# Feed-forward stage of a float32 decoder block: ACT, DVE and POOL in program order, with evacuations issued in steps and summed weight pages loaded from a list of their own

## The chip, the core and the metric

The kernel runs on one core of one Trainium2 chip. The metric is the device time of one execution in microseconds (us), smaller being better. Engines are named as in the profile: PE multiplies matrices (PEld is its weight load), DVE is the vector engine, ACT the scalar engine, POOL is GpSimd, and SP issues the DMAs.

## The reference

One decoder layer over 256 tokens of width 1024, all in float32: a mixer (8 block-sparse heads, of which at this length only the block of the token itself counts, and 4 differential heads, both gated), then a SwiGLU feed-forward of width 2816, each between two RMS norms.

```python
h = rms_norm(x, norm_mix_pre_g)
mq, mk, mv, dq, dk, dv, ga, gb = split(h @ w_in)
ya = moba_attention(mq, mk, mv)            # softmax with ALiBi, 8 heads of 64
yb = rms_norm(diff_attention(dq, dk, dv))  # softmax1 - lam * softmax2, 4 heads of 128
merged = sigmoid(ga) * (ya @ w_branch_a) + sigmoid(gb) * (yb @ w_branch_b)
x = x + rms_norm(merged @ w_out, norm_mix_post_g)
h = rms_norm(x, norm_ffn_pre_g)
f = (silu(h @ w_gate) * (h @ w_up)) @ w_down
x = x + rms_norm(f, norm_ffn_post_g)
```

## The kernel before

**Products.** Every float32 operand is kept as two parts, a rounded part `hi` and the rest `lo`, and every product is three matmuls into one PSUM bank: hi·hi, hi·lo, lo·hi (`mm3`, lines 216 to 218). So each weight tile of 128x1024, here called a granule, is first split (`split_part`): ACT writes `whi` (line 184), then DVE writes `wlo` = raw − `whi` (line 187). There are five buffers for `whi` and five for `wlo`. A granule's split therefore waits until PE is done with the granule five before it, and PE waits for both parts of a granule.

**Slots and jobs.** A stage is a list of slots. A slot holds a few matmuls (`pe`), the granules that they need, and what follows them (`post`). Splits and weight sums are jobs in one list. `run` walks the slots: it first issues all jobs up to those that slots a few places ahead need (`AHEAD` = 4 slots), then the matmuls, then `post`, then one step of every generator in `active`.

**Order on the engines.** PE and SP always run in program order. ACT, DVE and POOL run in program order inside the block that `order` opens. Outside it a scheduler at build time sets their order. Before, the scheduler orders them from the 15th slot of the mixer on, and in the whole feed-forward; program order holds at the start of the kernel and between the two stages.

**Feed-forward.** The 22 chunks of 128 hidden columns are computed in this order: 4 chunks as natural products (`nat`), then units `R 4, W 6, R 10, W 12, R 16, W 18`. An R unit covers 2 chunks with four granules r0 to r3, each used for both halves of the tokens (12 matmuls of 512 columns per granule). A W unit covers 4 chunks with seven block products in place of eight, on sums of weight blocks and of blocks of h. In PE's order its blocks are 21, 11, T2, T1, T3, 22 and T4, with two granules each and 6 matmuls per granule. The sums T1 to T4 are eight adds on DVE (line 268) over *pages* of 128x1024. The pages are loaded from HBM; twelve are in use, and a page is loaded anew when its last user is done. The sums of h (`s_step`: two adds, four half adds, two splits into `S`) are made once.

**From a unit to its down projection.** PE's result is evacuated from PSUM (R: SiLU on ACT, then a product on DVE, called `fr`, lines 1074 and 1075; W: `q1` to `q7`, ending in `f` of the first tokens, lines 1044 and 1045, and `f` of the second, lines 1049 and 1050). `f_T` transposes it on PE into the single bank `t` and splits the bank into `fT` hi (ACT) and `fT` lo (DVE). Then the down projection adds it into four `acc` banks: one granule per chunk, d0 to d21, 18 matmuls each (`z_slots`). PE's order in a unit is: first block or granule, transposes left over from the unit before, second block, down projection of the chunks before, the rest, and in a W unit the transposes of its first tokens. The last four chunks, d18 to d21, are split in halves and end the kernel (`z_tail`). Two of them have buffers of their own, named `wextra`.

In the mixer, `ev_q` and `ev_k` evacuate the q and k projections: DVE reads a bank of `acc` (four in turn, `q<-acc,R` at line 528), and ACT and DVE split the result. PE reuses the bank two slots later.

Of the kernel before, what the change touches and what calls it, by code (L numbers as in the profile page):

```python
# [20 lines left out]
F32 = mybir.dt.float32  # L21
F32R = mybir.dt.float32r
# [43 lines left out]
def tile_hybrid_block(  # L66
# [77 lines left out]
    def load_raw(r):  # L144
        if r["home"] == "page":
            r["page"] = free.pop(0)
            t = page(r["page"], "wpage")
        else:
            t = wpool.tile([P, 1024], F32, tag="raw", name="wraw", bufs=RB)
            raw_home.append(r)  # L150
        r["flat"] = t
        r["tile"] = t.rearrange("p (a c) -> p a c", a=r["a"])
        cur["raw"] += 1

    def load_raws():
        while cur["raw"] < len(raw_order):
            r = raw_order[cur["raw"]]
            if r["home"] == "page":
                if not free:
                    break  # L160
            elif len(raw_home) >= RB and raw_home[-RB]["uses"] > 0:
                break
            load_raw(r)
            for c, v in r["views"]:
                nc.sync.dma_start(r["tile"][:, :, c], v)
# [126 lines left out]
    for ui, (kind, f0) in enumerate(UNITS):  # L292
        ds = [lambda i=i: job_split(("d", i), dr[i]) for i in units_before(ui)]
        if kind == "R":
            rr = [raw_of([(slice(0, 256), rows(w_gate, 2 * kc * P, 2, f0 * P, 256)),
                          (slice(256, 512), rows(w_up, 2 * kc * P, 2, f0 * P, 256))], 2) for kc in range(4)]
            rs = [lambda kc=kc: job_split(("r", f0, kc), rr[kc]) for kc in range(4)]
            ad = early_sums(UNITS[ui + 1][1])
            todo = rs[0:2]
            if ui == 0:  # L300
                sjobs = [raw_of([], 2, "page") for i in range(4)]
                todo += [lambda: (use(*sjobs), [add_job(lambda n=n: s_step(n)) for n in range(10)])]
            for i in range(max(len(ds), 2)):
                todo += ds[i:i + 1] + ad[i:i + 1]
            ad = ad[max(len(ds), 2):]
            todo += rs[2:3] + ad[0:1] + rs[3:4] + ad[1:]
# [20 lines left out]
    def run(slots, ahead, starts={}):  # L327
        need = [max([job_of[h] for h in s["need"] if h in job_of], default=0) for s in slots]
        for i, s in enumerate(slots):
            split_to(max(need[:i + 1 + ahead(i)], default=0))  # L330
            for th in starts.get(i, []):
                active.append(th)
            s["pe"]()
            for f in s.get("post", []):
                f()
            for th in list(active):
                try:
                    next(th)
# [604 lines left out]
    mean_sq(xt[:, 1, :], ms2[:, 1:2])  # L943
    split_next()
    nat(fg[1], "gn", 1, range(4, 8))
    order.__exit__(None, None, None)
    rs2 = rstd(ms2, 2, NORM_EPS, "rs1")
    free.extend([10, 11, 12, 13])
    load_raws()
# [10 lines left out]

        return fT[f, t]

    def f_T(fv, f0, n, t, tag="t"):

        def pe():
            b = ps(tag)
            for j in range(n):
                nc.tensor.transpose(b[:, j * P:(j + 1) * P], fv()[:, j * P:(j + 1) * P], ident)
            h, l = [v[:, 0:n * P] for v in (work.tile([P, 512], F32R, tag="q", name="fT", bufs=5) for _ in range(2))] \
                if n == 4 else (lambda v: [v[:, 0:n * P], v[:, 256:256 + n * P]])(  # L970
                    work.tile([P, 512], F32R, tag="q", name="fT", bufs=5))
            split(b[:, 0:n * P], h, l)
            for j in range(n):
# [38 lines left out]
    def unit_W(f0):  # L1012
# [6 lines left out]

        def slots_of(n, bk, a, start, stop, post):  # L1020
            return [dict(pe=lambda kp=kp: block(bank(bk), a, n, f0, kp, start, stop), need=[((n, f0, kp), 0)],
                         post=[post] if kp else []) for kp in range(2)]

        def q1():
            s1 = work.tile([P, 512], F32, tag="ph0", name="s1", bufs=1)
            nc.scalar.activation(s1, st["a"], AF.Copy)
            g = st["g0"] = work.tile([P, 512], F32, tag="e", name="g0", bufs=4)
            nc.vector.tensor_tensor(g, st["b"], s1, op=OP.add)
            nc.scalar.activation(g, g, AF.Silu, scale=rs2[:, 0:1])

        def q6():
            st["s2"] = work.tile([P, 512], F32, tag="ph0", name="s2", bufs=1)
            nc.scalar.activation(st["s2"], st["a"], AF.Copy)

        def q5():
            st["v5"] = work.tile([P, 512], F32, tag="pl0", name="v5", bufs=1)
            nc.scalar.activation(st["v5"], st["b"], AF.Copy)

        def q7():
            nc.vector.tensor_tensor(st["v5"], st["v5"], st["a"], op=OP.subtract)  # L1040

        def q3():
            u = st["f0"] = work.tile([P, 512], F32, tag="e", name="f0", bufs=4)
            nc.vector.tensor_tensor(u, st["b"], st["s2"], op=OP.subtract)
            nc.vector.tensor_tensor(u, u, st["g0"], op=OP.mult)

        def q4():
            g = st["f1"] = work.tile([P, 512], F32, tag="e", name="f1", bufs=4)
            nc.scalar.activation(g, st["a"], AF.Silu, scale=rs2[:, 1:2])
            nc.vector.tensor_tensor(g, g, st["v5"], op=OP.mult)  # L1050

        head = slots_of("21", "b", A(0, 1), True, True, lambda: None)
# [4 lines left out]
        body[1].append(f_T(lambda: st["f0"], f0, 4, 0))  # L1057
        return head, body[0], body[1], [f_T(lambda: st["f1"], f0, 4, 1)]

    def unit_R(f0):  # L1060
        st = []
# [10 lines left out]
        def done(t):  # L1072
            g = st[t]["f"] = work.tile([P, 512], F32, tag="e", name="fr", bufs=4)[:, 0:256]
            nc.scalar.activation(g, st[t]["b"][:, 0:256], AF.Silu, scale=rs2[:, t:t + 1])
            nc.vector.tensor_tensor(g, st[t]["b"][:, 256:512], g, op=OP.mult)

        sl = [dict(pe=lambda kc=kc, t=t: pe(kc, t), need=[(("r", f0, kc), 0)],
                   post=[lambda t=t: done(t)] if kc == 3 else []) for kc in range(4) for t in range(NT)]
# [21 lines left out]
    slots[-1]["post"] = [nat_mul]  # L1100
    left = [f_T(lambda t=t: fgs[t], 0, 4, t, "pv" if t else "t") for t in range(NT)]
# [56 lines left out]
```

## Time and profile before

| | |
|---|---|
| median of 3 runs | 398.88 us (396.45 to 399.57) |
| the profiled execution | 399.47 us, span 397.7 us |
| PE busy | 375.9 us, 95% of the span |
| DVE busy | 311.1 us, 78% |
| ACT busy | 234.2 us, 59% |
| DMA | 67.64 MB, 170 GB/s on average |

The span runs from the first to the last instruction; the execution's own time is 1.8 us longer. The profiled execution lies 0.6 us above the median. The mixer takes the first 196 us, the feed-forward the rest. PE's busy time is nearly the span, so the place to read is PE's idle time, and what ended it.

### The profile page before, as it was taken

How to read it: one execution, taken by the hardware profiler on the slowest of the kernel's cores; microseconds unless marked ns; L12 is line 12 of the kernel's file. 1: busy time of each engine (PE TensorE's matmuls, PEld its weight loads, DVE VectorE, ACT ScalarE, POOL GpSimd, SP SyncE). 2: the span in 40 equal slices, each digit the busy share in tenths (PEclk: the TensorE clock that was granted, in tenths of full speed). 3: DMA queues.
4: the chain of work that ended last, by engine and by line, in shares of the span. 5: the costliest groups of instructions: out<-in, count | busy, mean ns of one | idle time of the engine just before them, and what ended most of it. 6: DMA issues, size and time to landing. Idle time of an engine off the chain costs nothing.

```text
span 397.7 us, 6046 instructions
## 1 busy us (share of the span) xinstructions
PE 375.9 (95%) x2212; PEld 326.8 (82%) x2212; DVE 311.1 (78%) x523; ACT 234.2 (59%) x402; POOL 34.0 (9%) x51
## 2 busy tenths in 40 slices
PE   7998999999999999999999997989998989979993
PEld 5798989998999999998888885867876868858883
DVE  2798787989877667896899996599866799677934
ACT  3964675777556864571786435675354763467721
POOL 0199600000000000000010000000000000000000
PEclk9999999999999999999999998999998999989999
DMA  6998555354455554685079923568451669000002
GB/s 197 388 298 296 161 162 160 105 158 136 129 158 160 194 177 159 199 270 168 14 274 370 380 70 110 160 211 264 160 155 48 188 227 356 33 0 0 2 0 106
DMA packets 37855, 67.64 MB, mean 170 GB/s; under 512 B 2993, under 2 KB 15298, under 8 KB 37826
## 3 DMA queue, kind: packets, MB, share of 16 engines
q1 hardware_dynamic: 37826, 67.26, 51.4%
q8 instruction: 17, 0.28, 0.3%
q14 instruction: 12, 0.10, 0.1%
HBM read 66.20 MB, written 1.05 MB: 169 GB/s over the span
## 4 chain that ended last, share of the span: by engine, by line
PE 82%; DVE 7%; DMA 6%; issue 2%; ACT 2%; SPq 1%; DVEq 0%; POOLq 0%; ACTq 0%
PE acc L216 13%; PE acc L217 13%; PE acc L218 13%; PE s L216 9%; PE s L217 8%; PE s L218 8%; PE acc L589 5%; DVE wlo L187 4%; DMA wpage<-in_w_up_dram 2%; DMA wpage<-in_w_gate_dram 2%; PE pv L217 2%; PE pv L218 2%; PE pv L216 2%; ACT whi L184 2%; DMA xt<-in_x_dram 1%
## 5 line engine op out<-in xcount | busy, mean ns | idle before, releaser
L187 DVE TENSOR_TENSOR wlo<-wraw,whi 128x1024 fp32r<-128x1024 f32 (+1 forms) x105 | 114.9, 1106 | 22.9 <-ACT whi L184 20.5
L184 ACT ACTIVATE whi<-wraw 128x1024 fp32r<-128x1024 f32 (+1 forms) x104 | 98.6, 962 | 57.5 <-PE acc L217 23.4
L216 PE MATMUL acc<-hTh,whi 128*128 128x256 f32 x256 | 73.4, 287 | 1.8 <-DVE q L528 1.6
L218 PE MATMUL acc<-hTh,wlo 128*128 128x256 f32 x256 | 71.9, 281 | 0.0
L217 PE MATMUL acc<-hTl,whi 128*128 128x256 f32 x256 | 71.9, 281 | 0.0
L187 DVE TENSOR_TENSOR wlo<-wpage,whi 128x1024 fp32r<-128x1024 f32 x42 | 50.6, 1223 | 18.9 <-ACT whi L184 18.8
L184 ACT ACTIVATE whi<-wpage 128x1024 fp32r<-128x1024 f32 x42 | 44.1, 1060 | 32.4 <-PE pv L218 18.7
L216 PEld LDWEIGHTS acc<-hTh,whi 128*128 128x128 f32 x256 | 48.3, 189 | 2.5 <-DVE q L528 1.8
L217 PEld LDWEIGHTS acc<-hTl,whi 128*128 128x128 f32 x256 | 48.3, 189 | 0.0
L218 PEld LDWEIGHTS acc<-hTh,wlo 128*128 128x128 f32 x256 | 48.2, 188 | 0.0
L216 PE MATMUL s<-whi,h2h 128*128 128x512 f32 x92 | 39.4, 428 | 2.7 <-DVE v L1040 1.6
L217 PE MATMUL s<-wlo,h2h 128*128 128x512 f32 x92 | 38.2, 416 | 0.0
L218 PE MATMUL s<-whi,h2l 128*128 128x512 f32 x92 | 38.0, 413 | 0.0
L268 DVE TENSOR_TENSOR wpage<-wpage 128x1024 f32<-128x1024 f32 x24 | 29.1, 1219 | 5.8 <-DMA wpage<-in_w_up_dram 4.3
L216 PE MATMUL acc<-whi,fT 128*128 128x512 f32 (+1 forms) x80 | 29.2, 365 | 0.0
L218 PE MATMUL acc<-whi,fT 128*128 128x512 f32 (+1 forms) x80 | 29.1, 364 | 0.0
L217 PE MATMUL acc<-wlo,fT 128*128 128x512 f32 (+1 forms) x80 | 29.1, 364 | 0.0
L216 PEld LDWEIGHTS s<-whi,h2h 128*128 128x128 f32 x92 | 18.4, 200 | 8.5 <-ACT whi L184 2.0
L852 POOL TENSOR_TENSOR rs_r<-rs_e,mhalf 128x1 f32<-128x1 f32 x4 | 2.2, 546 | 235.6 <-DVE rs_e L851 235.6
L218 PEld LDWEIGHTS s<-whi,h2l 128*128 128x128 f32 x92 | 18.3, 199 | 4.5
L217 PEld LDWEIGHTS s<-wlo,h2h 128*128 128x128 f32 x92 | 18.3, 199 | 3.6
L218 PE MATMUL s<-whi,S 128*128 128x512 f32 x48 | 19.0, 395 | 0.0
(267 smaller groups left out, 763.5 us busy)
## 6 DMA issues: line engine op xcount, KB each, us to landing
wraw<-in_w_in_dram SPq DMA_DIRECT2D x37, 512.0 KB, 3.7
wraw<-in_w_down_dram SPq DMA_DIRECT2D x22, 512.0 KB, 5.8
wpage<-in_w_up_dram SPq DMA_DIRECT2D x12, 512.0 KB, 4.1
wpage<-in_w_gate_dram SPq DMA_DIRECT2D x12, 512.0 KB, 7.5
wraw<-in_w_out_dram SPq DMA_DIRECT2D x8, 512.0 KB, 3.4
wraw<-in_w_gate_dram SPq DMA_DIRECT2D x12, 256.0 KB, 6.0
wraw<-in_w_up_dram SPq DMA_DIRECT2D x12, 256.0 KB, 6.1
wraw<-in_w_branch_a_dram SPq DMA_DIRECT2D x4, 512.0 KB, 3.5
```

The source lines that it names most:

```text
L184: nc.scalar.activation(hi, src, AF.Copy)
L187: nc.vector.tensor_tensor(lo, src, hi.bitcast(F32), op=OP.subtract)
L216: nc.tensor.matmul(dst, lh, rh, start=start, stop=False, **kw)
L217: nc.tensor.matmul(dst, lh, rl, start=False, stop=False, **kw)
L218: nc.tensor.matmul(dst, ll, rh, start=False, stop=stop, **kw)
L268: nc.vector.tensor_tensor(dst["flat"], a["flat"], b["flat"], op=OP.add)
L589: nc.tensor.matmul(acc[t], l[:, k, ts_], r, start=k == 0 and n == 0, stop=k == KT - 1 and n == 2)
L852: nc.gpsimd.tensor_tensor(r[:, 0:1], e, mhalf, op=OP.pow)
```

## The change

Four things change.

1. The block in which ACT, DVE and POOL run in program order no longer ends after the natural gate products, but at the end of the kernel. All of the feed-forward is now in program order on these engines.
2. Evacuations are generators. Each gives ACT its part, yields, and gives DVE its part one slot later. `f_T` issues transposes and the ACT copy in its own slot, does not step the others, and issues the DVE part after the next slot's matmuls. For an R unit the two halves of the tokens now share one bank and one pair of instructions (four transposes, one ACT copy and one DVE subtract of 512 columns), where there were two pairs of 256 before. Jobs are issued ahead by `granules_ahead`: up to six slots, but at most four granules that the slot itself does not use.
3. Pages have a list of their own (`page_order`); a page that is not free no longer holds back the raw tiles behind it. The sums of h are spread among the other jobs of the first unit.
4. All granules of `w_in` are split in two halves, where before only the first group was. This moves the scheduler's order in the mixer as well.

```diff
     def touch(r):
         if not r["there"]:
             r["there"] = True
-            raw_order.append(r)
+            (page_order if r["home"] == "page" else raw_order).append(r)
...
     def load_raws():
-        while cur["raw"] < len(raw_order):
...
+        while cur["raw"] < len(raw_order) and (len(raw_home) < RB or not raw_home[-RB]["uses"]):
+            load(raw_order[cur["raw"]])
+        while cur["page"] < len(page_order) and free:
+            load(page_order[cur["page"]])
...
-            job_split(("p", g, kc), raw1(w_in, kc * 2 * P, 2, g * 512, 512), (0, 1) if g == GROUPS[0] else None)
+            job_split(("p", g, kc), raw1(w_in, kc * 2 * P, 2, g * 512, 512), (0, 1))
...
+                todo = s_jobs(0) + rs[0:1] + s_jobs(1) + rs[1:2] + s_jobs(2, 3) + ds[0:1] + s_jobs(4, 5) + ds[1:2] + \
+                    s_jobs(6) + ds[2:3] + s_jobs(7, 8) + ds[3:4] + ad[0:1] + rs[2:3] + ad[1:3] + rs[3:4] + ad[3:]
+            else:
+                n = len(ds)
+                todo = rs[0:2] + [x for i in range(n) for x in ds[i:i + 1] + ad[i:i + 1]] + rs[2:3] + ad[n:n + 1] + \
+                    rs[3:4] + ad[n + 1:]
...
-            for th in list(active):
+            for th in list(active) if not s.get("short") else ():
...
+    def granules_ahead(slots, n, most):
+
+        def f(i):
+            j, seen = i + 1, set()
+            while j < len(slots) and j - i <= most:
+                seen |= {x for x, _ in slots[j]["need"]} - {x for x, _ in slots[i]["need"]}
+                if len(seen) > n:
+                    break
+                j += 1
+            return j - i - 1
+        return f
...
     nat(fg[1], "gn", 1, range(4, 8))
-    order.__exit__(None, None, None)
     rs2 = rstd(ms2, 2, NORM_EPS, "rs1")
...
-            split(b[:, 0:n * P], h, l)
-            for j in range(n):
-                fT[f0 + j, t] = [v[:, j * P:(j + 1) * P] for v in (h, l)]
-        return dict(pe=pe, need=[])
+            nc.scalar.activation(h, b, AF.Copy)
+            yield
+            nc.vector.tensor_tensor(l, b, h.bitcast(F32), op=OP.subtract)
+
+        def start():
+            th = pe()
+            next(th)
+            active.append(th)
+        return dict(pe=start, need=[], short=True)
...
         def q4():
             g = st["f1"] = work.tile([P, 512], F32, tag="e", name="f1", bufs=4)
             nc.scalar.activation(g, st["a"], AF.Silu, scale=rs2[:, 1:2])
+            yield
             nc.vector.tensor_tensor(g, g, st["v5"], op=OP.mult)
...
-        return sl[0:2], sl[2:4], sl[4:8], [f_T(lambda t=t: st[t]["f"], f0, 2, t) for t in range(NT)]
+                   post=[lambda t=t: active.append(done(t))] if kc == 3 else []) for kc in range(4) for t in range(NT)]
+        return sl[0:2], sl[2:4], sl[4:8], [f_T({t: (lambda t=t: st[t]["f"]) for t in range(NT)}, f0, 2)]
...
-    run(slots, lambda i: AHEAD)
+    run(slots, granules_ahead(slots, WB - 1, 6))
+    order.__exit__(None, None, None)
```

What this does to the engines' queues is shown at three places. In these rows a name ahead of `<-` is what is written, and `x2` means two such instructions in a row. No PE row moves: PE's list is the same before and after.

**From an R unit into a W unit, DVE.** The place is the end of unit R 4 and the start of unit W 6. `fr` is the R unit's result, `wlo<-wraw` the split of a down granule (d4, d5), `wlo<-wpage` that of a block of the W unit, `wpage<-wpage` a sum of pages, `fT` the low part of the transposed `fr`. Before:

```order
L1075 TENSOR_TENSOR fr<-s,fr 128x256 x2
L187 TENSOR_TENSOR wlo<-wraw,whi 128x1024 x2
L187 TENSOR_TENSOR wlo<-wpage,whi 128x1024
L223 TENSOR_TENSOR fT<-t,fT 128x256
L268 TENSOR_TENSOR wpage<-wpage 128x1024
L223 TENSOR_TENSOR fT<-t,fT 128x256
```

And after:

```order
L1117 TENSOR_TENSOR fr<-s,fr 128x256
L186 TENSOR_TENSOR wlo<-wraw,whi 128x1024
L1117 TENSOR_TENSOR fr<-s,fr 128x256
L267 TENSOR_TENSOR wpage<-wpage 128x1024
L186 TENSOR_TENSOR wlo<-wraw,whi 128x1024
L267 TENSOR_TENSOR wpage<-wpage 128x1024
L186 TENSOR_TENSOR wlo<-wpage,whi 128x1024
L999 TENSOR_TENSOR fT<-t,fT 128x512
```

The second `fr` now stands behind the split of d4, and the one `fT` behind two sums of pages and two splits; the same eight rows come again at W 12, and at W 18 with one split `wlo<-wpage` more ahead of `fT`.

**The end of the last W unit, DVE.** The place is unit W 18 and the first of the four last down granules. `v`, `f`, `f` are the first tokens' evacuation, the last `f` that of the second tokens, the 512-wide splits are halves of d18 to d21. Before:

```order
L1040 TENSOR_TENSOR v_3967<-v_3967,s 128x512
L187 TENSOR_TENSOR wlo<-wpage,whi 128x1024
L187 TENSOR_TENSOR wlo<-wraw,whi 128x512
L1044 TENSOR_TENSOR f_4002<-s,s_3945 128x512
L187 TENSOR_TENSOR wlo<-wraw,whi 128x512
L1045 TENSOR_TENSOR f_4002<-f_4002,g_3899 128x512
L187 TENSOR_TENSOR wlo<-wraw,whi 128x512 x2
L1050 TENSOR_TENSOR f_4017<-f_4017,v_3967 128x512
L223 TENSOR_TENSOR fT<-t,fT 128x512 x2
```

And after:

```order
L186 TENSOR_TENSOR wlo<-wpage,whi 128x1024 x6
L1078 TENSOR_TENSOR v_4029<-v_4029,s 128x512
L1083 TENSOR_TENSOR f_4064<-s,s_4007 128x512
L1084 TENSOR_TENSOR f_4064<-f_4064,g_3975 128x512
L186 TENSOR_TENSOR wlo<-wraw,whi 128x512 x2
L186 TENSOR_TENSOR wextra<-wraw,wextra 128x512 x2
L186 TENSOR_TENSOR wlo<-wraw,whi 128x512 x2
L186 TENSOR_TENSOR wextra<-wraw,wextra 128x512 x2
L1091 TENSOR_TENSOR f_4087<-f_4087,v_4029 128x512
L999 TENSOR_TENSOR fT<-t,fT 128x512 x2
```

`v` now stands behind all six splits of the blocks T3, 22 and T4, and the second tokens' `f` and both `fT` behind all eight halves, where the four `wextra` halves had been further up.

**The first evacuation of q in the mixer, DVE.** Here `q<-acc,R` frees a bank of `acc`, and `q<-q` is the split of q. Before:

```order
L528 TENSOR_TENSOR q<-acc,R_143 128x256
L187 TENSOR_TENSOR wlo<-wraw,whi 128x1024
L223 TENSOR_TENSOR q<-q 128x256
L528 TENSOR_TENSOR q<-acc,R_143 128x256 x2
L511 TENSOR_TENSOR lam<-lexp 128x1
L512 TENSOR_SCALAR lam<-lam 128x1
L187 TENSOR_TENSOR wlo<-wraw,whi 128x1024
L223 TENSOR_TENSOR q<-q 128x256 x2
L528 TENSOR_TENSOR q<-acc,R_143 128x256
```

And after:

```order
L551 TENSOR_TENSOR q<-acc,R_143 128x256 x2
L186 TENSOR_TENSOR wlo<-wraw,whi 128x512
L222 TENSOR_TENSOR q<-q 128x256 x2
L551 TENSOR_TENSOR q<-acc,R_143 128x256 x2
L186 TENSOR_TENSOR wlo<-wraw,whi 128x512
```

The fourth evacuation of a bank no longer stands behind a whole split and two splits of q.

## Rows read from the trace of the kernel before

**Rows 1.** Page, head and busy time: us (share of the span) and instructions

```profile
span 397.7 us, 6046 instructions
PE 375.9 (95%) x2212; PEld 326.8 (82%) x2212; DVE 311.1 (78%) x523; ACT 234.2 (59%) x402; POOL 34.0 (9%) x51
```

**Rows 2.** Waits of PE, whole span: us in total, times, longest us

```profile
PE t L968 <- DVE fT L223: 7.6, 3, 2.5
PE acc L216 <- DVE q L528: 1.6, 1, 1.6
PE s L216 <- DVE v L1040: 1.6, 1, 1.6
PE s L216 <- ACT whi L184: 1.1, 1, 1.1
...
PE t L968 <- DVE f L1045: 0.9, 2, 0.4
PE pv L656 <- DVE ya L223: 0.6, 1, 0.6
PE acc L216 <- DVE kf L536: 0.2, 1, 0.2
```

**Rows 3.** Timeline of PE, 241 to 250 us: start, us, instruction [idle before]

```profile
241.73 0.38 PE L968 MATMUL t<-ident,fr 128*128 128x128 f32 x2
244.63 0.44 PE L968 MATMUL t<-ident,fr 128*128 128x128 f32 x2 [2.52 <-DVE fT L223]
...
246.58 0.63 PE L216 MATMUL s<-whi,h2h 128*128 128x512 f32 x1
247.01 0.63 PE L217 MATMUL s<-wlo,h2h 128*128 128x512 f32 x1
```

**Rows 4.** Windows: PE, PEld, DVE, ACT, POOL busy, clock granted, DMA

```profile
70.00:100.00 30.00, 29.19 (x235) 28.27 (x234) 28.10 (x77) 22.21 (x54) 0.00 (x0) 1.00 0.45 138
204.00:234.00 30.00, 30.00 (x147) 24.94 (x146) 30.00 (x33) 18.34 (x21) 1.63 (x1) 1.00 0.82 298
```

**Rows 5.** Timeline of DVE, rows of several places

```profile
35.88 0.41 DVE L528 TENSOR_TENSOR q<-acc,R 128x256 f32<-128x256 f32 x1
...
209.35 3.49 DVE L187 TENSOR_TENSOR wlo<-wraw,whi 128x1024 fp32r<-128x1024 f32 x3
...
239.42 0.42 DVE L1075 TENSOR_TENSOR fr<-s,fr 128x256 f32<-128x256 f32 x1 [0.65 <-ACT fr L1074]
...
256.96 1.23 DVE L268 TENSOR_TENSOR wpage<-wpage 128x1024 f32<-128x1024 f32 x1 [2.37 <-DMA wpage<-in_w_up_dram]
...
378.15 0.68 DVE L223 TENSOR_TENSOR fT<-t,fT 128x512 fp32r<-128x512 f32 x1
```

**Rows 6.** Timeline of ACT, rows of several places

```profile
21.30 3.89 ACT L184 ACTIVATE whi<-wraw 128x1024 fp32r<-128x1024 f32 x4
...
238.91 0.47 ACT L1074 ACTIVATE fr<-s,rs 128x256 f32<-128x256 f32 x1 [0.92 <-PE s L218]
...
354.96 1.15 ACT L184 ACTIVATE wextra<-wraw 128x512 fp32r<-128x512 f32 x2 [1.02 <-DVE wlo L187]
...
376.82 0.69 ACT L1049 ACTIVATE f<-s,rs 128x512 f32<-128x512 f32 x1 [1.65 <-PE s L218]
377.40 0.59 ACT L222 ACTIVATE fT<-t 128x512 fp32r<-128x512 f32 x1
```

**Rows 7.** Timeline of PE, rows of several places

```profile
222.13 0.40 PE L216 MATMUL acc<-whi,fT 128*128 128x512 f32 x1
222.37 0.40 PE L217 MATMUL acc<-wlo,fT 128*128 128x512 f32 x1
...
224.89 0.39 PE L216 MATMUL acc<-whi,fT 128*128 128x512 f32 x1
...
376.62 0.60 PE L968 MATMUL t<-ident,f 128*128 128x128 f32 x4
376.97 0.47 PE L216 MATMUL acc<-whi,fT 128*128 128x512 f32 x1
```

More of the change, by code (lines that the diff above doesn't have):

```diff
@@ L108, in tile_hybrid_block @@
     gran, jobs, job_of, extra, place = {}, [], {}, [], {}
-    raw_order, raw_home, free = [], [], []
-    cur = dict(raw=0, job=0, extra=0)
+    raw_order, page_order, raw_home, free = [], [], [], []
+    cur = dict(raw=0, page=0, job=0, extra=0)
     def raw_of(views, a, home="raw"):
@@ L152, in load_raw, with load @@
         r["tile"] = t.rearrange("p (a c) -> p a c", a=r["a"])
-        cur["raw"] += 1
+        cur[r["home"]] += 1
     def load_raws():
-        while cur["raw"] < len(raw_order):
[L157 to L165, printed above, removed]
+        while cur["raw"] < len(raw_order) and (len(raw_home) < RB or not raw_home[-RB]["uses"]):
+            load(raw_order[cur["raw"]])
+        while cur["page"] < len(page_order) and free:
+            load(page_order[cur["page"]])
+    def load(r):
+        load_raw(r)
+        for c, v in r["views"]:
+            nc.sync.dma_start(r["tile"][:, :, c], v)
     def granule(n):
@@ L298, in tile_hybrid_block, with s_jobs, f, touch_s @@
             ad = early_sums(UNITS[ui + 1][1])
-            todo = rs[0:2]
             if ui == 0:
                 sjobs = [raw_of([], 2, "page") for i in range(4)]
[L302 to L306, printed above, removed]
+                def s_jobs(*ns):
+                    def f():
+                        if ns[0] == 0:
+                            touch_s()
+                        for n in ns:
+                            add_job(lambda n=n: s_step(n))
+                    return [f]
+                def touch_s():
+                    use(*sjobs)
+                todo = s_jobs(0) + rs[0:1] + s_jobs(1) + rs[1:2] + s_jobs(2, 3) + ds[0:1] + s_jobs(4, 5) + ds[1:2] + \
[4 more added lines that the diff above has]
+                    rs[3:4] + ad[n + 1:]
         else:
@@ L961, in f_of, with f_T @@
         return fT[f, t]
-    def f_T(fv, f0, n, t, tag="t"):
+    def f_T(fvs, f0, n, tag="t"):
         def pe():
             b = ps(tag)
-            for j in range(n):
[L968 to L971, printed above, removed]
-            split(b[:, 0:n * P], h, l)
-            for j in range(n):
-                fT[f0 + j, t] = [v[:, j * P:(j + 1) * P] for v in (h, l)]
-        return dict(pe=pe, need=[])
+            w = [(i, t, j) for i, t in enumerate(fvs) for j in range(n)]
+            for i, t, j in w:
+                c = (i * n + j) * P
+                nc.tensor.transpose(b[:, c:c + P], fvs[t]()[:, j * P:(j + 1) * P], ident)
+            h, l = [work.tile([P, 512], F32R, tag="q", name="fT", bufs=5) for _ in range(2)]
+            for i, t, j in w:
+                c = (i * n + j) * P
+                fT[f0 + j, t] = [v[:, c:c + P] for v in (h, l)]
+            nc.scalar.activation(h, b, AF.Copy)
[6 more added lines that the diff above has]
+        return dict(pe=start, need=[], short=True)
     Sp = [page(14 + i, "S", F32R).rearrange("p (r k q) -> p r k q", r=2, k=4) for i in range(4)]
@@ L1021, in slots_of, with q2 @@
             return [dict(pe=lambda kp=kp: block(bank(bk), a, n, f0, kp, start, stop), need=[((n, f0, kp), 0)],
-                         post=[post] if kp else []) for kp in range(2)]
+                         post=[lambda: active.append(post())] if kp else []) for kp in range(2)]
+        def q2():
+            return
+            yield
         def q1():
@@ L1026, in q1 @@
             nc.scalar.activation(s1, st["a"], AF.Copy)
+            yield
             g = st["g0"] = work.tile([P, 512], F32, tag="e", name="g0", bufs=4)
             nc.vector.tensor_tensor(g, st["b"], s1, op=OP.add)
+            yield
             nc.scalar.activation(g, g, AF.Silu, scale=rs2[:, 0:1])
@@ L1033, in q6 @@
             nc.scalar.activation(st["s2"], st["a"], AF.Copy)
+            yield
         def q5():
@@ L1037, in q5 @@
             nc.scalar.activation(st["v5"], st["b"], AF.Copy)
+            yield
         def q7():
             nc.vector.tensor_tensor(st["v5"], st["v5"], st["a"], op=OP.subtract)
+            yield
         def q3():
@@ L1045, in q3 @@
             nc.vector.tensor_tensor(u, u, st["g0"], op=OP.mult)
+            yield
         def q4():
@@ L1049, in q4 @@
             nc.scalar.activation(g, st["a"], AF.Silu, scale=rs2[:, 1:2])
+            yield
             nc.vector.tensor_tensor(g, g, st["v5"], op=OP.mult)
-        head = slots_of("21", "b", A(0, 1), True, True, lambda: None)
+        head = slots_of("21", "b", A(0, 1), True, True, q2)
         body = slots_of("11", "a", A(0, 0), True, True, q1), [
@@ L1056, in unit_W @@
                         ("T4", "a", A(1, 1), False, True, q4)) for s in slots_of(*x)]
-        body[1].append(f_T(lambda: st["f0"], f0, 4, 0))
-        return head, body[0], body[1], [f_T(lambda: st["f1"], f0, 4, 1)]
+        body[1].append(f_T({0: lambda: st["f0"]}, f0, 4))
+        return head, body[0], body[1], [f_T({1: lambda: st["f1"]}, f0, 4)]
     def unit_R(f0):
@@ L1074, in done @@
             nc.scalar.activation(g, st[t]["b"][:, 0:256], AF.Silu, scale=rs2[:, t:t + 1])
+            yield
             nc.vector.tensor_tensor(g, st[t]["b"][:, 256:512], g, op=OP.mult)
         sl = [dict(pe=lambda kc=kc, t=t: pe(kc, t), need=[(("r", f0, kc), 0)],
-                   post=[lambda t=t: done(t)] if kc == 3 else []) for kc in range(4) for t in range(NT)]
-        return sl[0:2], sl[2:4], sl[4:8], [f_T(lambda t=t: st[t]["f"], f0, 2, t) for t in range(NT)]
+                   post=[lambda t=t: active.append(done(t))] if kc == 3 else []) for kc in range(4) for t in range(NT)]
+        return sl[0:2], sl[2:4], sl[4:8], [f_T({t: (lambda t=t: st[t]["f"]) for t in range(NT)}, f0, 2)]
     def nat_slots():
@@ L1087, in nat_slots, with nat_mul, nat_silu @@
                 for kc in range(4) for t in range(NT)]
-    def nat_mul():
-        for t in range(NT):
-            nc.vector.tensor_tensor(fgs[t], fu[t], fgs[t], op=OP.mult)
+    def nat_mul(t):
+        nc.vector.tensor_tensor(fgs[t], fu[t], fgs[t], op=OP.mult)
     zb.clear()
     fgs = []
-    for t in range(NT):
+    def nat_silu(t):
         g = work.tile([P, NAT * P], F32, tag="e", name="fgs", bufs=4)
@@ L1099, in tile_hybrid_block @@
     slots = nat_slots()
-    slots[-1]["post"] = [nat_mul]
-    left = [f_T(lambda t=t: fgs[t], 0, 4, t, "pv" if t else "t") for t in range(NT)]
+    for t in range(NT):
+        slots[t]["post"] = [lambda t=t: nat_silu(t)]
+        slots[t - NT]["post"] = [lambda t=t: nat_mul(t)]
+    left = [f_T({t: lambda t=t: fgs[t]}, 0, 4, "pv" if t else "t") for t in range(NT)]
     for i, (kind, f0) in enumerate(UNITS):
```

## The prediction, made before the changed kernel ran

> **What bounds the kernel now.** The head of the page comes first: PE is busy for 375.9 of 397.7 us [rows 1], so all that the change can give back is PE's idle time and PE's slow time. The list of PE's waits names the idle time [rows 2]. In the mixer it is 1.6 us for an evacuation of q, and 0.6 and 0.2 us around 93 us, 2.4 in all. In the feed-forward it is 7.6 us in three waits of 2.5 (the second pair of transposes of an R unit waits until DVE has read the single bank `t`), 1.6 and 1.1 us inside W units, and 0.9 us ahead of the transposes of `f`: 11.2 in all. The timeline shows what follows a wait of 2.52 us [rows 3]: soon after it, matmuls of 512 columns start 0.43 us apart, where 0.235 is usual [rows 7]. That is the lower of the clock's two levels, 1.2 in place of 2.4 GHz. Eight matmuls run so, 8 x 0.195 = 1.55 us, once behind each of the three waits: 4.65 us. After the wait of 1.6 us in the mixer the clock stays up. So 2.4 + 11.2 + 4.65 = 18.25 us is the most that can be won.
>
> DVE is the engine that PE waits for. It is full for 30 us as the feed-forward starts, and 94% busy between 70 and 100 us [rows 4]. What counts is therefore which DVE instruction stands ahead of the one that PE waits for.
>
> **Prices.** On DVE, splits of 1024 columns follow one another every 1.14 us (three end after 3.49, the last result 0.08 late); 512 columns take 0.60 and a `fr` of 256 takes 0.34, their 0.68 and 0.42 less the same 0.08 [rows 5]. On ACT they take 0.95 and 0.53, a SiLU or `fr` releases the next instruction after some 0.58 and 0.37, and ACT starts 0.20 after PE's last matmul has made way (376.82 against 376.62) [rows 6, 7]. A granule takes PE 12 x 0.235 = 2.8 us in an R unit, 1.4 in a W unit, 2.76 in the down projection, and four transposes 0.35, with 0.1 to start again [rows 7]. PE's own list does not change, so each place can be laid out with these.
>
> **What it removes.** The two pairs of transposes share a bank: the three waits of 2.5 us go, and the low clock behind them. In W units, v was late because a sum of pages stood ahead of it and waited for its DMA (2.37 us of idle DVE in one row) [rows 5]; in program order the sums stand in the R unit, when pages have long landed, and the 1.6 and 1.1 go. `f` and its product now stand in a row (the 0.9 goes). In the mixer the fourth q evacuation comes behind two half splits in place of a full one and two splits of q, about 2 us earlier than the wait needs: from 35.88 [rows 5] to about 34. I count 2.0 of the 2.4 us as won, and up to 2.4. Removed: 11.2 + 4.65 + 2.0 = 17.85 us.
>
> **What it adds: waits for what stands ahead of `fT` on DVE.** The third matmul of each triple needs the low part, so PE gets two matmuls (0.47) into the down projection before it stops.
>
> *R to W.* Count from the end of r3 on PE. ACT: second `fr` at 0.20, then the split of the down granule from 0.57 to 1.63. DVE: that split to 2.79, second `fr` to 3.2, sum 4.3, split 5.4, sum 6.55, split 7.7, `fT` done 8.4. PE: two granules of 21 to 2.8, waits for `fr` until 3.2, transposes and block 11 to 6.5, two matmuls to 7.0, waits until 8.4. Loss 0.4 + 1.4 = 1.8, also at W 12. At W 18 one split more stands ahead, 1.14: 2.95. Sum 6.55.
>
> *W to R.* Count from the end of T4. ACT takes the SiLU of the second `f` (0.20 to 0.78), then the split of the next down granule to 1.84; DVE does that split to 3.0, `f` to 3.6, `fT` of the first tokens to 4.3. Only then is bank `t` free. PE has done transposes and r0 by 3.25: 1.05 lost. The second `fT` then stands behind two sums and two splits (4 x 1.14) and is done at 9.45; PE needs it at 8.75: 0.7. Two such places: 3.5.
>
> *First unit.* DVE waits in order for the natural products, then has 0.75 + 1.2 + 1.14 + 1.2 + 3 x 1.14 + 0.7 = 8.4 us of work up to the first `fT`; PE needs 2.8 + 0.8 + 2.9 + 0.47 = 7.0 for r0, the transposes, r1 and two matmuls: 1.4.
>
> *Inside W 18.* d17 is split before T2 but used after T4, so one of five buffers is held. T4's second split on ACT then ends 2.2 us after T3's last matmul (two splits behind it), DVE's 1.2 later, and v behind it 0.7: 4.1 against 2.8 that block 22 covers: 1.3.
>
> *The end.* From the end of T4: SiLU 0.78, `fT` hi 1.26, first `wextra` half 1.88; then DVE has six halves (3.6), `f` (0.6) and `fT` (0.7): 6.75 before bank `t` is free. PE has transposed and done d17 by 3.2: 3.55. Before, two of the halves stood in the W unit, and nothing waited here.
>
> Idle time added: 6.55 + 3.5 + 1.4 + 1.3 + 3.55 = 16.3 us. The last two long ones, 2.5 at W 18 and 3.55 at the end, are as long as those that were followed by the low clock: 2 x 1.55 = 3.1. The shorter ones are nearer to the 1.6 that was not. Added: 19.4.
>
> Edits with one answer: the page list moves loads earlier, and pages are needed later than they land, so it costs and gives nothing by itself; if a page were late by 2 us, a sum would stop DVE and the W-to-R terms grow by as much. POOL's few instructions in the feed-forward are off this path. The 36 `w_in` granules in halves cost DVE 0.06 each (2 x 0.60 - 1.14), 2.2 us in all, under PE's work as long as DVE has slack, which between 70 and 100 us is 1.9 us; bounds of the mixer are therefore +2.2 and -2.4, and I take -2.0 since the one large wait lies at 36 us, away from the full stretch.
>
> Of that edit the Trainium skill (Perfetto Trace Analysis, Optimizing Scalar/DVE Operations) says two things: breaking up instructions may let work end sooner if the engine isn't saturated but causes bubbles, and grouping helps if it is saturated. The first is the wait at 36 us; the second speaks against the edit at 70 to 100 us. By the page's 60 ns for each DVE instruction the estimate is 2.2 us too, and if the second rule ruled, the sum below would be 404.6.
>
> **The sum.** 399.47 - 17.85 + 19.4 = 401.0 us for an execution like the profiled one; that one lies 0.6 above the median, so 400.4. The gain is turned into other waits for the same engine.
>
> **The rivals.**
> *Saturated mixer.* The 0.06 us per granule lie fully on the path and the wait at 36 us stays in another form: 400.4 + 2.0 + 2.2 = 404.6. It decides from the point at which DVE's slack of 1.9 us per 30 is used up; against it, by the trace 8 of the 36 granules fall in that stretch. 0.08.
> *The clock falls at shorter waits.* At W 6, W 12 and the first unit PE idles 1.4 to 1.8 us, in one or two pieces. The trace shows no fall at 1.6 and a fall at 2.5; if it falls from 1.8 down, 2 or 3 x 1.55 are added: 403.5 to 405. Slower than before. 0.18.
> *The clock stays up.* It does not fall at W 18 and at the end: 400.4 - 3.1 = 397.3. Against it: the same length fell three times in three. 0.12.
> *The waits do not add up.* Each is laid out from a PE event as if DVE entered it without a lead. If the lead that DVE gains in one PE wait shortens the next, only the largest of each unit counts: W 18, first unit and end stay (7.9), W 6, W 12, W to R and v go (3.6 + 3.5 + 1.3 = 8.4): 392. For it: DVE idles inside W units before [rows 5]. Against it: each chain starts with an ACT instruction that waits for that very PE event. 0.14.
>
> **How the numbers follow.** My case has 0.48, with its own range of 398 to 403. About 1%, 4 us, is what a measurement of this kernel can tell from no change. Faster than 394.9 comes from the last rival and a little of the third, 0.17; slower than 402.9 from the first two and the edge of my case, 0.28; the rest is 0.55. The range must reach into both sides: 394.5 to 404.5.
>
> **What would show it.** In the changed profile: no wait of `t<-ident,fr` for `fT`; new waits of `acc<-whi,fT` for DVE `fT` of 1.4, 1.4 and 2.5 us; waits of `t<-ident,f` for DVE `fT` of 1.0 twice and of 3.5 at the end; low clock after the last two; no wait for q at 36 us. I am wrong if PE's list of waits in the feed-forward sums to well under 11 us, or if the mixer does not end some 2 us ahead of its 196.

## The result, and the profile of the changed kernel

The changed kernel takes 400.26 us (median of 19 runs, 398.07 to 403.04); the kernel before, timed beside it, 398.45 us (19 runs, 395.00 to 401.01). The ratio is 1.0066, 95% interval 1.0039 to 1.0093: slower, by less than one per cent. The forecast was 400.4. The profiled execution took 402.57 us with a span of 400.8, so it lies near the upper end of its runs.

The head of the page of the changed kernel, and the granted clock of its 40 slices (in tenths of full speed, one digit a slice):

```profile
PE 376.9 (94%) x2212; PEld 326.6 (81%) x2212; DVE 312.0 (78%) x556; ACT 235.6 (59%) x435; POOL 31.5 (8%) x51
...
PEclk9899999999999999999999999999999999989979
```

PE does the same work as before, and DVE nearly the same, in 33 more instructions and 0.9 us more [rows 1]. The list of PE's waits of the changed kernel (us in total, times, longest):

```profile
PE acc L217 <- DVE fT L999: 7.6, 6, 2.6
PE t L992 <- DVE fT L999: 5.4, 3, 3.5
PE s L455 <- DMA xt<-in_x_dram: 1.9, 1, 1.9
...
PE s L215 <- DVE v L1078: 0.6, 1, 0.6
PE acc L215 <- DVE q L551: 0.4, 1, 0.4
PE s L215 <- DVE fr L1117: 0.4, 1, 0.4
```

Against [rows 2], the three waits of 2.5 us for bank `t`, the waits for v and whi and those for `f` are gone, and 13.0 us of waits for `fT` are there. One by one on PE's timeline (start, us, instruction, idle time before it and what ended that):

```profile
222.94 0.50 PE L217 MATMUL acc<-whi,fT 128*128 128x512 f32 x1 [1.49 <-DVE fT L999]
239.77 0.49 PE L215 MATMUL s<-whi,h2h 128*128 128x512 f32 x1 [0.38 <-DVE fr L1117]
247.64 0.50 PE L217 MATMUL acc<-whi,fT 128*128 128x512 f32 x1 [1.10 <-DVE fT L999]
...
276.27 0.50 PE L217 MATMUL acc<-whi,fT 128*128 128x512 f32 x1 [0.52 <-DVE fT L999]
300.32 0.50 PE L217 MATMUL acc<-whi,fT 128*128 128x512 f32 x1 [1.44 <-DVE fT L999]
...
354.22 0.50 PE L217 MATMUL acc<-whi,fT 128*128 128x512 f32 x1 [2.58 <-DVE fT L999]
370.53 0.47 PE L215 MATMUL s<-whi,h2h 128*128 128x512 f32 x1 [0.56 <-DVE v L1078]
380.29 1.12 PE L992 MATMUL t<-ident,f 128*128 128x128 f32 x4 [3.50 <-DVE fT L999]
...
383.34 0.63 PE L217 MATMUL acc<-whi,fT 128*128 128x512 f32 x1
383.77 0.63 PE L215 MATMUL acc<-wextra,fT 128*128 128x512 f32 x1
```

The places are those of the prediction: first unit, W 6 (two pieces), W to R, W 12, W 18, v, the end. The last two rows show the low clock, a granted clock of 0.5: 0.43 us from start to start. What PE waits for at the end stands on DVE's timeline of the same stretch:

```profile
362.66 7.12 DVE L186 TENSOR_TENSOR wlo<-wpage,whi 128x1024 fp32r<-128x1024 f32 x6 [1.75 <-ACT whi L183]
369.70 0.68 DVE L1078 TENSOR_TENSOR v<-v,s 128x512 f32<-128x512 f32 x1
...
375.33 1.29 DVE L186 TENSOR_TENSOR wextra<-wraw,wextra 128x512 fp32r<-128x512 f32 x2 [2.42 <-ACT wextra L183]
376.55 1.29 DVE L186 TENSOR_TENSOR wlo<-wraw,whi 128x512 fp32r<-128x512 f32 x2
377.75 1.28 DVE L186 TENSOR_TENSOR wextra<-wraw,wextra 128x512 fp32r<-128x512 f32 x2
378.95 0.68 DVE L1091 TENSOR_TENSOR f<-f,v 128x512 f32<-128x512 f32 x1
379.56 0.68 DVE L999 TENSOR_TENSOR fT<-t,fT 128x512 fp32r<-128x512 f32 x1
```

Six halves, then the product, then the `fT` that frees bank `t`: DVE idles for 2.42 us ahead of work that nobody is waiting for yet, and does the wanted work behind it.

The windows of [rows 4] for the changed kernel (busy us of PE, PEld, DVE, ACT, POOL, the clock granted, DMA share, GB/s):

```profile
70.00:100.00 30.00, 30.00 (x244) 29.39 (x244) 28.37 (x85) 23.17 (x63) 0.00 (x0) 1.00 0.36 118
204.00:234.00 30.00, 28.51 (x139) 23.40 (x139) 27.09 (x29) 16.33 (x19) 0.00 (x0) 1.00 0.89 312
```

In the mixer PE is full from 70 to 100 us although DVE has 0.3 us more to do. At the start of the feed-forward DVE was full before and now idles for 2.9 of 30 us.

### The profile page after: what moved, and what is told of

Read it like the earlier page. It is cut to its first block, busy times and chain, and to the rows that moved or that the text cites. A ratio compares the mean times of both kernels' runs of the same rounds, so it can differ in the third digit from the quotient of the medians.

```text
span 400.8 us, 6146 instructions
## 1 busy us (share of the span) xinstructions
PE 376.9 (94%) x2212; PEld 326.6 (81%) x2212; DVE 312.0 (78%) x556; ACT 235.6 (59%) x435; POOL 31.5 (8%) x51
## 4 chain that ended last, share of the span: by engine, by line
PE 75%; DVE 11%; issue 5%; DMA 4%; ACT 4%; SPq 1%; DVEq 0%; POOLq 0%; ACTq 0%
PE acc L217 13%; PE acc L215 12%; PE acc L216 12%; PE s L215 7%; PE s L216 7%; PE s L217 7%; DVE wlo L186 5%; PE acc L612 4%; DMA wraw<-in_w_in_dram 3%; ACT whi L183 2%; PE pv L216 2%; PE pv L217 2%; PE pv L215 2%; DVE wpage L267 2%; DVE fT L999 1%
## 5 line engine op out<-in xcount | busy, mean ns | idle before, releaser
L186 DVE TENSOR_TENSOR wlo<-wraw,whi 128x512 fp32r<-128x512 f32 (+1 forms) x141 | 119.2, 868 | 29.4 <-ACT whi L183 29.1
L183 ACT ACTIVATE whi<-wraw 128x512 fp32r<-128x512 f32 (+1 forms) x140 | 101.6, 763 | 43.4 <-PE acc L216 14.5
L215 PE MATMUL s<-whi,h2h 128*128 128x512 f32 x92 | 37.6, 409 | 0.9 <-DVE v L1078 0.6
L217 PE MATMUL acc<-whi,fT 128*128 128x512 f32 (+1 forms) x80 | 30.6, 382 | 7.6 <-DVE fT L999 7.6
L216 PE MATMUL s<-wlo,h2h 128*128 128x512 f32 x92 | 36.4, 396 | 0.0
L217 PE MATMUL s<-whi,h2l 128*128 128x512 f32 x92 | 36.4, 395 | 0.0
L215 PE MATMUL acc<-whi,fT 128*128 128x512 f32 (+1 forms) x80 | 30.1, 377 | 0.0
L217 PEld LDWEIGHTS acc<-whi,fT 128*128 128x128 f32 x80 | 15.6, 195 | 12.7 <-DVE fT L999 10.2
L215 PEld LDWEIGHTS s<-whi,h2h 128*128 128x128 f32 x92 | 17.3, 188 | 6.0 <-DVE fr L1117 1.6
L217 PEld LDWEIGHTS s<-whi,h2l 128*128 128x128 f32 x92 | 17.3, 188 | 4.2
L216 PEld LDWEIGHTS s<-wlo,h2h 128*128 128x128 f32 x92 | 17.3, 188 | 3.4
```

The source lines that it names most:

```text
L183: nc.scalar.activation(hi, src, AF.Copy)
L186: nc.vector.tensor_tensor(lo, src, hi.bitcast(F32), op=OP.subtract)
L215: nc.tensor.matmul(dst, lh, rh, start=start, stop=False, **kw)
L216: nc.tensor.matmul(dst, lh, rl, start=False, stop=False, **kw)
L217: nc.tensor.matmul(dst, ll, rh, start=False, stop=stop, **kw)
```

## The experiments

The numbers of each are the median, and the ratio to the kernel before in runs on the same chip with its 95% interval.

**halves_only.** The kernel before with the mixer's part alone:

```
-job_split(("p", g, kc), raw1(...), (0, 1) if g == GROUPS[0] else None)
+job_split(("p", g, kc), raw1(...), (0, 1))
```

> The kernel before with one part of the change alone: all w_in granules of the mixer split in halves of 512. Theory: PE's wait of 1.63 us for q at 36 us becomes 0.4 or less, the two small waits at 93 to 95 us go too, the feed-forward keeps its three waits of 2.5 us: about 2.0 to 2.6 us less than before, ratio 0.994. Rival (the added 0.06 us per granule lies on the path): 2.2 us more, ratio 1.0055.

Measured: 396.62 us, ratio 0.9953 (0.9917 to 0.9988). PE's waits:

```profile
PE t L968 <- DVE fT L223: 7.6, 3, 2.5
PE s L216 <- DVE v L1040: 2.4, 2, 1.4
...
PE acc L216 <- DVE q L528: 0.4, 1, 0.4
```

The wait for q is 0.4 in place of 1.63, those at 93 to 95 us are gone, and the feed-forward keeps its three. The rival is out: the halves give 1.8 us by the medians.

**ffn_only.** The changed kernel with that line as before, so the feed-forward's part alone.

> The changed kernel with the mixer's w_in granules unsplit as before (only the first group in halves), so the feed-forward's part alone. Theory: the wait for q at 36 us is back, so 2.0 to 2.6 us more than the changed kernel, about 402.5, ratio to before 1.011. Rival (the halves cost time): 398, ratio 0.999.

Measured: 403.12 us, ratio 1.0117 (1.0070 to 1.0164). The wait of 1.63 us for q is back, the feed-forward's waits are those of the changed kernel to 0.02 us, but for one of 0.23 us in W 18 that is new. So the change is a gain of some 2 us in the mixer and a loss of some 4.7 us in the feed-forward.

**shared_bank.** The kernel before, ACT and DVE still in the scheduler's order, with one edit: the transposes of an R unit go to one bank.

```
-return ..., [f_T(lambda t=t: st[t]["f"], f0, 2, t) for t in range(NT)]
+return ..., [f_T2({t: (lambda t=t: st[t]["f"]) for t in range(NT)}, f0, 2)]
```

`f_T2` makes four transposes into one `t` and one `split` of 512 columns.

> The kernel before with only the transposes of R units changed: both pairs write one PSUM bank, one ACT copy and one DVE subtract of 512 columns evacuate them; ACT and DVE order stays the scheduler's. Theory: the three waits of 2.5 us and the low clock behind them go (7.6 + 4.65 us) and nothing takes their place, because only three splits stand ahead of fT on DVE there (fT is done some 5.5 us after the last matmul of the unit, PE wants it after 6.5): 386 to 388, ratio 0.97. Rival (what stands on DVE must be done anyway, so the wait moves to fT or to the next granule): 394 to 399.

Measured: 386.81 us, ratio 0.9710 (0.9656 to 0.9764). DVE's timeline behind the R unit:

```profile
239.15 0.42 DVE L1090 TENSOR_TENSOR fr<-s,fr 128x256 f32<-128x256 f32 x1 [0.65 <-ACT fr L1089]
240.10 2.49 DVE L187 TENSOR_TENSOR wlo<-wraw,whi 128x1024 fp32r<-128x1024 f32 x2 [0.53 <-ACT whi L184]
242.76 1.22 DVE L187 TENSOR_TENSOR wlo<-wpage,whi 128x1024 fp32r<-128x1024 f32 x1 [0.17 <-ACT whi L184]
243.90 0.68 DVE L223 TENSOR_TENSOR fT<-t,fT 128x512 fp32r<-128x512 f32 x1
244.50 1.22 DVE L268 TENSOR_TENSOR wpage<-wpage 128x1024 f32<-128x1024 f32 x1
```

Three splits stand ahead of `fT`, and it is done 0.1 us before PE's first down matmul (244.70). No wait is left there and no low clock. The page sum stands behind `fT`; in the changed kernel two sums stand ahead of it. So the shared bank alone gives 11.6 us, and the changed kernel has lost that again; evac_first shows by what.

**evac_first.** The changed kernel with the three evacuations issued one step earlier, the amount of work unchanged. This is the edit in `f_T`; `done` and `q4` lose their `yield` in the same way:

```
 nc.scalar.activation(h, b, AF.Copy)
-yield
 nc.vector.tensor_tensor(l, b, h.bitcast(F32), op=OP.subtract)
```

> The changed kernel with three evacuations issued one step earlier in DVE's program order: the low part of fT, the products fr and f of the second tokens come right behind their ACT instruction, ahead of the splits and sums that the next step looks ahead to; amount of work unchanged. Theory: DVE's order is the whole loss; the waits for fT of 1.5 (first unit), 1.1 and 0.4 (W 6), 1.4 (W 12), 0.5 twice and the 3.5 at the end go, 0.95 twice falls to about 0.4, 2.6 at W 18 falls to about 1.5, and the low clock at the end goes: 385 to 389, ratio 0.97. Rival (DVE is the bound over the whole stretch, so the same time returns as waits for whi or wlo of the granules): 397 to 400.

Measured: 387.33 us, ratio 0.9711 (0.9649 to 0.9773). PE's waits:

```profile
PE s L215 <- DVE fr L1112: 2.2, 1, 2.2
...
PE acc L217 <- DVE fT L998: 1.2, 1, 1.2
...
PE t L992 <- DVE fT L998: 0.7, 2, 0.4
```

Of 13.0 us of waits for `fT` 1.9 are left, with the same instructions on the same engines, still in program order. So what costs the time is where the evacuations stand in that order, and not program order as such. The number of steps that jobs are issued ahead and the new places of the sums were not changed alone by any run. In the first R unit the rival holds, however: the wait of 1.5 for `fT` came back as 2.2 for `fr`, with low clock (0.5) behind it. DVE's timeline there:

```profile
211.59 0.69 DVE L1127 TENSOR_TENSOR fgs<-t,fgs 128x512 f32<-128x512 f32 x1 [1.39 <-PE t L217]
212.99 0.69 DVE L1127 TENSOR_TENSOR fgs<-pv,fgs 128x512 f32<-128x512 f32 x1 [0.71 <-PE pv L217]
213.59 1.41 DVE L1025 TENSOR_TENSOR wpage<-wpage 128x512 f32<-128x512 f32 x2
...
233.22 4.63 DVE L186 TENSOR_TENSOR wlo<-wpage,whi 128x1024 fp32r<-128x1024 f32 x4
237.76 0.75 DVE L1112 TENSOR_TENSOR fr<-s,fr 128x256 f32<-128x256 f32 x2
```

DVE works from 212.99 to 238.5 without a gap, and idles 1.39 + 0.71 us right ahead of it.

**nat_later.** evac_first with the natural products issued two steps later, so that other work fills those 2.1 us (`a` are the first two slots of the first unit):

```
-slots[t - NT]["post"] = [lambda t=t: nat_mul(t)]
+a[t]["post"] = [lambda t=t: nat_mul(t)]
```

> evac_first with the two natural products of the first unit issued two steps later, behind two half sums of S and a split; nothing else moves on DVE. Theory: from the natural products to the first fr DVE works without a gap there, and the 1.39 + 0.71 us that it idles in front of the products are the same time as PE's wait of 2.24 us for fr; so that wait falls to 0.2 or less, and the low clock behind it goes too: 387.3 less 2.0 to 3.6, so 383.7 to 385.3. Rival (fr is late since its place on DVE was moved, or through ACT): the wait stays, 387.

Measured: 384.60 us, ratio 0.9648 (0.9571 to 0.9725). PE's wait:

```profile
PE s L215 <- DVE fr L1112: 0.9, 1, 0.9
```

It is 0.91 in place of 2.24, and the clock stays up behind it. The time is as expected, but 0.7 us more of the wait is left than I had put. The interval overlaps with that of evac_first, so it is the trace that shows the wait shrink; the 2.7 us between the medians are less sure.

**tail_only.** The changed kernel with the edit of evac_first in the last unit alone, for `f1` and `fT` (`if f0 != UNITS[-1][1]: yield`).

> The changed kernel with only the last unit's product f1 and its fT issued one step earlier on DVE, ahead of four or six of the halves of the last down granules. Theory: the wait of 3.50 us for bank t at the end goes, and the low clock behind it (1.55 to 2.5 us): 394 to 395.3, ratio 0.99. Rival (the halves have to be split anyway, so PE waits for wextra or wlo instead): 398 to 400.

Measured: 394.94 us, ratio 0.9914 (0.9886 to 0.9941). DVE's timeline at the end:

```profile
373.35 0.69 DVE L1093 TENSOR_TENSOR f<-f,v 128x512 f32<-128x512 f32 x1 [1.42 <-ACT f L1090]
373.96 0.68 DVE L1000 TENSOR_TENSOR fT<-t,fT 128x512 fp32r<-128x512 f32 x1
374.56 1.28 DVE L186 TENSOR_TENSOR wextra<-wraw,wextra 128x512 fp32r<-128x512 f32 x2
```

The product and the first `fT` now stand ahead of the six halves. The wait at the end is gone and no wait for `wextra` or `wlo` takes its place. Against the changed kernel that is 5.3 us by the medians, 6.1 by the two ratios, for two instructions that stood six halves too late.

**one_list.** The changed kernel with raw granules and pages in one load list, as before (`raw_order.append(r)` for both).

> The changed kernel with raw granules and pages in one load list again, as before. Theory: in the changed order the sums stand in R units, and pages have landed by then either way, so nothing: 400.3, within 1 us. Rival (the list of its own is what makes program order bearable): sums wait for pages on DVE and the waits for fT grow, 403 to 408.

Measured: 399.02 us, ratio 1.0036 (1.0002 to 1.0070), which overlaps with that of the changed kernel. Each wait for `fT` is within 0.07 us of the one it had. The list of its own gives nothing here; whether it costs up to 1 us is not settled.

**bank_halves and bank_halves_pages.** shared_bank with the halves, and both with the page list as well.

> The kernel before with two parts of the change: R units' transposes in one bank, and all w_in granules in halves. Theory: the two gains add up, since one lies in the mixer and the other in the feed-forward: 386.8 less 1.8 to 2.5, so 384.3 to 385.0. Rival (the halves cost time once DVE has less slack): 387 or more.

> The same, and the pages of the sums loaded from a list of their own as in the change. Theory: the waits of 1.1 to 1.5 us for v and whi in W units come from sums that wait for their pages, so they go: 2.6 us less than with the two parts, about 382. Rival (these waits come from DVE's own work ahead of v): no change, 384 to 385.

Measured: 383.92 us, ratio 0.9661 (0.9604 to 0.9718), and 382.97 us, 0.9638 (0.9585 to 0.9692). By the medians the two gains add up, though the first interval overlaps with that of shared_bank; in the profile of bank_halves the three waits of 2.5 us and those at 93 to 95 us are gone, and 0.5 us are left of the wait for q. For the page list the theory fell: the intervals overlap, and DVE's timeline reads alike. bank_halves:

```profile
251.67 1.23 DVE L268 TENSOR_TENSOR wpage<-wpage 128x1024 f32<-128x1024 f32 x1 [0.97 <-DMA wpage<-in_w_up_dram]
...
259.62 0.68 DVE L1055 TENSOR_TENSOR v<-v,s 128x512 f32<-128x512 f32 x1
```

and bank_halves_pages:

```profile
251.53 1.23 DVE L267 TENSOR_TENSOR wpage<-wpage 128x1024 f32<-128x1024 f32 x1 [1.03 <-DMA wpage<-in_w_up_dram]
...
259.48 0.68 DVE L1054 TENSOR_TENSOR v<-v,s 128x512 f32<-128x512 f32 x1
```

A list of its own doesn't make the page land earlier: the sum waits 1 us for it either way, and v is at the same place.

**both.** nat_later with d17 ahead of T2 (`slots += a + left + b + zs + c + nxt`).

> nat_later with both slots of d17 in W 18 ahead of T2 in place of behind T4 (PE's own order changes by one granule). Theory of the prediction (d17 holds one of five buffers and so delays T4's split and v): the wait of 0.57 us for v goes, and 0.2 for g may; 0.6 to 0.8 us less than nat_later. Rival (v stands behind six splits that DVE runs without a gap): the wait for v stays at 0.4 or more, or moves, and the time is within 0.5 us of nat_later, or up to 2.8 us more since block transposes of f1 then have no down granule to cover them.

Measured: 386.61 us, ratio 0.9683 (0.9618 to 0.9747). PE's waits:

```profile
PE t L992 <- DVE fT L998: 3.9, 3, 3.1
```

The waits for `fT` (1.2), g (0.2) and v (0.55) of W 18 are gone, and 3.1 us stand at the end, where d17 had covered the six halves, with low clock behind. Two microseconds were moved, not won. The run doesn't tell whether the buffer that d17 holds or the 2.8 us of PE work that it puts ahead of T2 took the first three away.

**best.** both with two edits at the end (`last` is the first slot behind the last `f_T`):

```
+far = granules_ahead(slots, WB - 1, 6)
-run(slots, granules_ahead(slots, WB - 1, 6))
+run(slots, lambda i: far(i) if i >= last else min(far(i), last - i))
-[f_T({1: lambda: st["f1"]}, f0, 4)]
+[f_T({1: lambda: st["f1"]}, f0, 4, "s" if f0 == UNITS[-1][1] else "t")]
```

> The kernel called both, with two edits at its end: the look-ahead doesn't go past the last transposes until they are issued (so two halves in place of six stand ahead of f1 and fT on DVE), and the last transposes of f1 go to a bank of tag s, which is free there, in place of t. Theory: the wait of 3.14 us at the end falls to the 1.1 us that SiLU and product of f1 take after T4 (0.78 + 0.7 less 0.45 of other transposes), and the low clock behind it (1.6 us) goes: 386.6 less 3.6, so 382.5 to 383.5. Rival (the halves are then late for the last down granules): 385 to 387, with waits for wextra or wlo.

Measured: 383.35 us (382.85 to 383.93), ratio 0.9630 (0.9599 to 0.9661). PE's waits:

```profile
PE s L992 <- DVE f L1087: 1.1, 1, 1.1
...
PE acc L216 <- DVE wextra L186: 0.3, 1, 0.3
```

The 1.1 that was worked out is there, and the halves are late by 0.3. The two edits were not run apart. This program order and bank_halves_pages, in the scheduler's order, come out within 0.4 us of each other, 15 us below the kernel before.

## Why the prediction was right, and where it was not

Set the same PE instruction of both traces side by side (PE's list is the same, so the nth matmul is the nth): the difference of their starts, after less before, moves at each wait, and the steps are what a term cost on the path. They are larger than the idle times by up to 0.25 us for each wait; that PE needs this to start again is likely, but no run shows it apart.

| term | predicted, us | measured idle | measured step |
|---|---|---|---|
| start (x from DMA, low clock) | 0 | +0.8 | +1.4 |
| mixer: q, kf, ya | -2.0 | -2.05 | -2.6 |
| feed-forward: waits removed, and low clock | -15.85 | -11.2 and clock | -16.2 |
| first unit | +1.4 | 1.49 | 1.54 |
| R to W, W 6 | +1.8 | 0.38 + 1.10 | 1.76 |
| R to W, W 12 | +1.8 | 1.44 | 1.59 |
| R to W, W 18 | +2.95 | 2.58 | 2.74 |
| W to R, two places | +3.5 | 2 x (0.95 + 0.52) | 3.66 |
| v (and g) in W 18 | +1.3 | 0.56 | 1.18 |
| end | +3.55 | 3.50 | 3.9 |
| low clock behind W 18 and the end | +3.1 | | 1.65 + 2.45 |
| sum | +1.55 | | +3.1 |

The sum of the steps is the difference of the two spans, 400.8 - 397.7. It is 1.55 us more than predicted, and 1.4 of that is the start, which belongs to this execution: the load of x ended PE's wait after 1.88 us in place of 1.09, and low clock followed. The change hardly moves that load: four of its five pieces are issued at the same times in both traces, the last 0.2 us later. In the other profiles that wait is between nothing and 1.9 us. So the median hardly holds it in full, though no execution at the median was profiled. The idle time added in the feed-forward was put at 16.3 us and measured 14.0, the low clock was put too short, and the start at nothing: the misses go both ways, so that the forecast of 400.4 met 400.26 to 0.1 us is luck.

*What it removes* held: shared_bank shows the part of the bank, halves_only that of the mixer. The sign set for the mixer, an end some 2 us ahead of its 196, is not met in this profile as it stands: it ends 1.2 us ahead, 1.4 us late from the start less the 2.6 us won. *What it adds* held place by place, and evac_first and tail_only show its cause: which instruction stands ahead of the wanted one on DVE. In the R to W places each wait was 0.3 to 0.4 us shorter than laid out: the wait of 0.4 for `fr` hardly shows at W 12 and W 18, and block 21 takes PE 2.9 us and not 2.8. *First unit* was right in size, but its price was only half of the case: evac_first shows that DVE is the bound there, so the order behind the products didn't win the 1.5 us; filling the idle time ahead of them won a part (nat_later).

*Inside W 18* failed in its reasoning. d17 was to keep T4's second split on ACT back. In the trace ACT has done that split at 368.3, and DVE gets to it at 368.6: v stands at the end of six splits that DVE runs without a gap from 362.66 on. The buffer was held one step earlier (ACT idles 5.24 us up to 358.00 for PE's last down matmul). So the size was half of what I had put, 0.56, and the rest of the step is 0.36 at the block that starts at 364.1. In the run called both, all waits of W 18 went with d17's place, so the order there costs 2 us in some way; the part of it that is the buffer stays open.

*The end* was right in size: 3.50 for 3.55. But before the change six of the eight halves, and not two, had been split when T4 ended; only the last two (376.23) were left.

*The clock* held for both places, with 2.45 in place of 1.55 at the end, where all matmuls up to 386 us run at the lower level. That a wait of 2.5 us is always followed by the low clock was too strong (below): the rival in which the clock stays up came true at W 18 in the profile of one_list (398.76 us). Of the changed kernel, the fastest of the 19 runs (398.07 us) had a mean granted clock of 0.997, the profiled one 0.982, so its runs differ in this too.

*The page list* gives nothing by itself, as put: one_list. That v was late before because a sum ahead of it waited for its page is not shown: with the page list the sum waits just as long for its page, and v is no earlier. What the changed kernel shows is only that v is in time at W 6 and W 12 with the sums in R units.

*The rivals.* Saturated mixer: out, the halves gain 1.8 us (halves_only), and without them the changed kernel's ratio is 1.0117 in place of 1.0066 (ffn_only; these two intervals overlap), though DVE's busy time from 70 to 100 us rose from 28.10 to 28.37. Those 0.27 us are less than the 0.48 that eight granules in halves add by the prediction's 0.06 each. The Trainium skill (Perfetto Trace Analysis, Optimizing Scalar/DVE Operations) says that breaking up instructions may let work end sooner where the engine isn't saturated but causes bubbles on others. The trace of halves_only agrees, with 1.2 us less of PE's wait for q. Clock at shorter waits: out, no wait up to 1.6 us in the feed-forward of any of these traces was followed by it. The waits don't add up: out, they stood side by side.

## What to carry to other kernels

Before an engine is put in program order, list for every instruction that the critical engine waits for what the look-ahead issues ahead of it on its own engine; work for later must be issued behind the evacuation, not ahead of it. Two instructions that stood behind six halves for later cost 5 to 6 us here, and a part of a change that gives 12 us alone (the shared bank) came out as a loss together with another. When a wait goes, ask whether the engine behind it had a gap at all: where it had none, the wait comes back under another name, and the gap to fill lies ahead of it.

## What the runs showed of the chip that was not expected

The same wait on PE is not always followed by the low clock. Windows of halves_only around its three waits of 2.52 us (the clock granted is the third number from the end):

```profile
242.00:250.00 8.00, 6.18 (x31) 5.21 (x32) 6.12 (x8) 4.25 (x8) 0.00 (x0) 1.00 0.11 17
296.00:304.00 8.00, 6.41 (x32) 5.41 (x33) 6.05 (x7) 4.26 (x7) 0.00 (x0) 1.00 0.12 27
350.00:358.00 8.00, 6.94 (x26) 5.66 (x27) 4.09 (x7) 4.60 (x7) 0.00 (x0) 0.79 0.00 0
```

and of one_list around its waits of 2.57 and 3.50 us:

```profile
350.00:360.00 10.00, 7.21 (x34) 5.66 (x34) 5.62 (x7) 4.03 (x6) 0.00 (x0) 1.00 0.00 0
376.00:386.00 10.00, 8.46 (x32) 6.90 (x33) 2.99 (x6) 1.88 (x5) 0.00 (x0) 0.83 0.00 1
```

In the feed-forward of all profiled executions, waits of 2.52 to 2.58 us were followed by the low level (1.2 GHz) in 7 of 10 cases, those of 3.1 to 3.5 in 4 of 4, one of 2.24 (evac_first) was, and none of 1.6 or less. At the start waits of 1.87 and 1.88 us were, and those of 1.76 and less were not. How long PE waits is therefore not all that decides; what else does stays open. The time of a run also goes with its clock: the 19 runs of the changed kernel go from 398.07 us at a mean granted clock of 0.997 to 403.04 at 0.982, some 0.32 us for each 0.001, and best, which has no long wait, stays within 1.1 us at 0.996 to 0.999. A wait of this length can cost more than its idle time, and a profile shows one draw of it.
